# A diffusion layer in float32 on one core: its first phase written in a fixed order, some modulation chunks left unsplit, tiles given places

## The chip, the core and the metric

The kernel runs on one core of a Trainium2 chip. A core has a matmul engine (TensorE, PE in the profile; its weight loads are listed apart as PEld), two engines for element-wise work (VectorE, DVE, and ScalarE, ACT), a general engine (GpSimd, POOL) and an engine that here only issues DMA loads (SyncE, SP). Matmul results land in PSUM, which has 8 banks of 512 float32 columns; everything else lies in SBUF, 128 partitions wide. The metric is the time of one execution in microseconds on the device; less is better.

## What is computed

One layer over 256 latent tokens `x` and 256 context tokens `ctx`, width 2048, in float32, cut to what matters here:

```python
mod = silu(c) @ w_mod + b_mod                      # 6 x 2048 values; mod_c the same of c_ctx
sa, ca, ga, sm, cm, gm = split(mod, 6)
h   = rmsnorm(x)   * nw * (1 + ca)   + sa          # latent tokens
h_c = rmsnorm(ctx) * nw * (1 + ca_c) + sa_c        # context tokens
q, k, v, pool_in, gate_logits = h @ w_in           # of h_c only keys and values
q, k = rope(rmsnorm(q)), rope(rmsnorm(k))          # 16 half heads of 64
heads = (softmax(q1 k1) - lam * softmax(q2 k2)) @ v    # 8 heads, latent queries, all keys
y_a = rmsnorm(heads) @ w_a_up
y_b = (window means of 2, 4, 8, 16 tokens of pool_in - pool_in) @ pool_w @ w_b_up
x = x + ga * ((sigmoid(g_a) * y_a + sigmoid(g_b) * y_b) @ w_o)
x = x + gm * (relu(modulate(x, sm, cm) @ w_ff1) ** 2 @ w_ff2)
```

The first phase needs the parts `sa` and `ca` of the modulation, for both conditioning vectors at once, ahead of h and h_c.

## The kernel before

**Split products.** A float32 product is made from three matmuls in a faster, shorter format (f32r): each operand is split into a high and a low half, and high x high, high x low and low x high are summed in PSUM (`mm3`, lines 241 to 243). A 512 KB chunk of weights (128 x 1024) therefore goes through a chain: SP loads it into `raw` (5 buffers), ACT casts it to `whi` (line 213, 3 buffers), DVE subtracts to get `wlo` (line 214, 3 buffers), PE uses both. The order of all chunks is a list, `stream`, filled by `plan`; `wchunk` hands out the next one and keeps two more under way. 128 chunks of the later modulation parts bypass this: DVE multiplies them into a sum (`late_part`, line 588).

**First phase (0 to 171 us).** `w_m0` (2 x 4 chunks) and seven stretches of 8 chunks `w_m` give the modulation: the weights stream past `cv`, a stationary tile that holds silu(c) and silu(c_ctx) in halves in 4 of its 128 columns, so 4 rows of `mod` result (`mod_chunk`, line 347). After a stretch the rows are copied (`mod_rows`, line 352), turned into columns (`mod_columns`, line 359), combined with the biases in four DVE operations, and `hidden` makes tiles of h or h_c: per 256 columns a DVE scaling (line 380), an ACT addition that gives the high half (381), a DVE difference that gives the low half (382). Sums of squares for the two norms come from ACT, an addition (line 460; on DVE for x, on POOL for the context) and a matmul (461). Between the chunks stand steps of the first half of keys (4 tiles of 128 tokens) and of queries (2 tiles): a step is the three matmuls of one tile and one 128-row slice. Keys for h, queries and keys for h_c are separate generators that the table `carried` puts behind given chunks; the chunk of keys is kept in `first` until the context has used it too. Loads are in the order prm, x (4), `w_m0`, then chunks and context between.

**After it.** `qk_evac` normalizes and rotates keys and queries (POOL's sum at line 440) and queues a turn, the transposes of line 447, a given number of chunks later (`later`, `tick`). Then values group 0 (to about 210), queries, keys, values of group 1 (to 356), the pooling input `pin` (window sums on POOL, line 744; edges and difference in `pool_diff`, lines 756 to 760), gates `pg`/`pyy` (to 704), `w_o`, and the MLP in blocks (850 to 1512). `xstat` (lines 410 to 413) is the matmul loop with tokens stationary. In `pin`, the first ff1 block and ff1 (lines 939 and 942) it is the other way round: 128 columns of the weight chunk are the stationary side, tokens stream, 512 columns (both halves of h, line 939) or 256 (line 942). Attention is a side generator that the loop `run` advances by the matmuls counted (`scores` line 646, softmax 647 to 657, transposes 665, products with the values 674). A recording layer orders each engine's instructions as PSUM banks and buffers come free; `pin` keeps marked ones in the order of the code.

## Time and profile before

| | |
|---|---|
| median of 3 executions | 1519.9 us (1519.45 to 1520.57) |
| the profiled execution | 1519.78 us, its span 1517.7 us |
| outside the span | 2.1 us |
| PE / DVE / ACT / POOL busy | 98% / 70% / 50% / 9% |
| DMA, mean over the span | 229 GB/s |
| first phase | 0 to 171 us, with 17 matmuls of the values at its end |

The profile comes from the profiled execution; times in it are in us from the start of its span. A row of windows gives a stretch, its length, and for each engine the busy time with the count, then the clock that PE was granted (1 is full), the share of DMA time and the rate. A row of groups gives line, engine, operation, output and input tiles, shapes, count, busy time and mean ns of one, and the idle time before with what ended it. A timeline row gives the start, the duration, the operation and, in brackets, the wait ahead of it. Matmuls overlap: one of 512 columns takes some 390 ns from end to end while the next starts 227 ns after it.

### The profile page before, as it was taken

What the parts mean: (1) busy time and instruction counts of PE and PEld (TensorE: products, weight loads), DVE (VectorE), ACT (ScalarE), POOL (GpSimd) and SP (SyncE); (2) the same over time, 40 slices, a digit from 0 to 9 for tenths busy, and PEclk for the clock granted to TensorE, in tenths of its full rate; (3) what the DMA queues carried; (4) which work ended last, traced back from release to release, by engine and by line L of the source; (5) the groups of instructions that cost most, each with busy time, mean ns of one, the idle gap of its engine ahead of it and who ended that gap; (6) DMA issues with size and microseconds to landing.
All of it is one profiled execution on the core that took longest, in us unless ns stands there. A gap on an engine that the chain in (4) does not pass through costs nothing.

```text
span 1517.7 us, 19767 instructions
## 1 busy us (share of the span) xinstructions
PE 1480.7 (98%) x7336; PEld 1232.8 (81%) x7336; DVE 1063.2 (70%) x1280; ACT 755.7 (50%) x1007; POOL 129.3 (9%) x124
## 2 busy tenths in 40 slices
PE   7899999999989999999999999999999999999998
PEld 5677877768878888888879988888888888888887
DVE  7799878777887767666757665666666555555675
ACT  6677534556655444444444554544444454444432
POOL 0100111000140000000000100100000000000170
PEclk9899999999999999999999999999999999999999
DMA  8888668556568787788755677767777666666664
GB/s 314 310 283 308 214 215 285 177 167 193 167 216 300 254 275 272 242 295 296 235 181 168 220 251 245 232 217 244 231 241 240 202 188 193 193 187 193 184 200 142
DMA packets 97439, 347.82 MB, mean 229 GB/s; under 512 B 11072, under 2 KB 11712, under 8 KB 97344
## 3 DMA queue, kind: packets, MB, share of 16 engines
q1 hardware_dynamic: 96768, 345.49, 70.4%
q8 instruction: 57, 0.93, 0.3%
q0 software_dynamic: 576, 1.08, 0.2%
q14 instruction: 38, 0.31, 0.1%
HBM read 344.44 MB, written 2.10 MB: 228 GB/s over the span
## 4 chain that ended last, share of the span: by engine, by line
PE 88%; issue 3%; DVE 3%; DMA 3%; ACT 1%; POOL 1%; DVEq 0%; SPq 0%; ACTq 0%; POOLq 0%
PE f L939 14%; PE f L411 8%; PE f L410 8%; PE f L413 8%; PE f L942 7%; PE pg L413 4%; PE pg L410 4%; PE pg L411 4%; PE pyy L410 2%; PE wo L410 2%; PE wo L413 2%; PE wo L411 2%; PE pyy L413 2%; PE pyy L411 2%; PE v L411 2%
## 5 line engine op out<-in xcount | busy, mean ns | idle before, releaser
L214 DVE TENSOR_TENSOR wlo<-raw,whi 128x1024 fp32r<-128x1024 f32 x507 | 628.6, 1244 | 365.2 <-ACT whi L213 350.9
L213 ACT CAST whi<-raw 128x1024 fp32r<-128x1024 f32 x507 | 529.8, 1047 | 587.3 <-PE f L411 178.1
L939 PE MATMUL f<-h,whi 128*128 128x512 f32 x896 | 224.2, 392 | 0.0
L411 PE MATMUL f<-whi,act 128*128 128x512 f32 x512 | 199.3, 389 | 0.0
L410 PE MATMUL f<-whi,act 128*128 128x512 f32 x512 | 199.3, 389 | 0.0
L939 PEld LDWEIGHTS f<-h,whi 128*128 128x128 f32 x896 | 161.5, 189 | 29.1
L588 DVE SCALAR_TENSOR_TENSOR macc<-raw,sil,macc 128x1024 f32<-128x1024 f32 x128 | 166.2, 1299 | 1.4 <-DMA raw<-in_w_cm_dram 0.8
L413 PE MATMUL f<-wlo,act 128*128 128x512 f32 x512 | 136.8, 389 | 0.0
L942 PEld LDWEIGHTS f<-h,wlo 128*128 128x128 f32 x896 | 122.2, 190 | 8.7
L942 PE MATMUL f<-h,wlo 128*128 128x256 f32 x896 | 124.9, 282 | 0.0
L413 PEld LDWEIGHTS f<-wlo,act 128*128 128x128 f32 x512 | 96.1, 188 | 20.0
L411 PEld LDWEIGHTS f<-whi,act 128*128 128x128 f32 x512 | 96.1, 188 | 19.8
L410 PEld LDWEIGHTS f<-whi,act 128*128 128x128 f32 x512 | 96.1, 188 | 19.8
L410 PE MATMUL pg<-whi,hL 128*128 128x512 f32 x256 | 100.5, 393 | 0.0
L411 PE MATMUL pg<-whi,hL 128*128 128x512 f32 x256 | 99.7, 389 | 0.0
L950 POOL TENSOR_TENSOR rsq<-relu 128x512 f32<-128x512 f32 x28 | 29.2, 1042 | 537.6 <-ACT relu L949 516.7
L413 PE MATMUL pg<-wlo,hL 128*128 128x512 f32 x256 | 68.6, 390 | 2.5 <-DVE wlo L214 2.5
L413 PEld LDWEIGHTS pg<-wlo,hL 128*128 128x128 f32 x256 | 48.0, 188 | 12.9 <-DVE wlo L214 2.9
L410 PEld LDWEIGHTS pg<-whi,hL 128*128 128x128 f32 x256 | 48.1, 188 | 10.1 <-issue 0.2
L411 PEld LDWEIGHTS pg<-whi,hL 128*128 128x128 f32 x256 | 48.1, 188 | 10.1 <-issue 0.2
L410 PE MATMUL wo<-whi,mix 128*128 128x512 f32 x128 | 49.9, 390 | 0.0
L411 PE MATMUL wo<-whi,mix 128*128 128x512 f32 x128 | 49.8, 389 | 0.0
(267 smaller groups left out, 2205.1 us busy)
## 6 DMA issues: line engine op xcount, KB each, us to landing
raw<-in_w_ff_dram SPq DMA_DIRECT2D x240, 512.0 KB, 4.3
raw<-in_w_m_dram SPq DMA_DIRECT2D x64, 512.0 KB, 4.9
raw<-in_w_ga_dram SPq DMA_DIRECT2D x32, 512.0 KB, 4.6
raw<-in_w_cm_dram SPq DMA_DIRECT2D x32, 512.0 KB, 4.6
raw<-in_w_gb_in_dram SPq DMA_DIRECT2D x32, 512.0 KB, 4.5
raw<-in_w_ga_in_dram SPq DMA_DIRECT2D x32, 512.0 KB, 4.4
raw<-in_w_sm_dram SPq DMA_DIRECT2D x32, 512.0 KB, 4.7
raw<-in_w_o_dram SPq DMA_DIRECT2D x32, 512.0 KB, 4.6
```

Source lines behind the costliest of these rows:

```text
L213: act.copy(hi, raw)
L214: vec.tensor_sub(lo, raw, hi.bitcast(F32))
L410: pe.matmul(banks[t], tok(h, k, 0, tt), wt, start=k == 0, stop=False)
L411: pe.matmul(banks[t], tok(h, k, 1, tt), wt, start=False, stop=False)
L413: pe.matmul(banks[t], tok(h, k, 0, tt), wt, start=False, stop=k == 2 * nk - 1)
L588: pin(vec.scalar_tensor_tensor(acc, raw, sil[:, 0, k:k + 1], acc, ALU.mult, ALU.add))
L939: pe.matmul(ps, hi[:, kk * P:kk * P + P], both(h2, k), start=k == 0, stop=False)
L942: pe.matmul(ps[:, T:2 * T], lo[:, kk * P:kk * P + P], act_slice(h2, k, 0), start=False, stop=k == KT - 1)
L950: gp.tensor_mul(sq, r, r)
```

## The change

It rewrites the first phase and moves a few steps behind it.

1. All four engines and SP keep the order of the code until the phase ends (`ordered_all`). Tables say what follows which chunk: `STRETCHES` (loads), `then` (rows, turns, columns, hidden tiles, squares, tables), `PACE` (steps of keys and queries). Steps come from one queue, `side`, 96 in all. `w_m0`'s first half is loaded ahead of x; the context's squares are added on DVE.
2. In each stretch one chunk (two in the first three), ten in all, is not split: its float32 weights are used as they are, 4 matmuls of 256 columns, with the 2 columns of `sil` (float32) as the stationary side.
3. `scale_stream` multiplies x or the context in place by its norm, 512 columns at once; `hidden` then has one ACT operation per 256 columns with scale and bias, one ACT cast and one DVE subtraction for 512 columns, the latter after the next chunk (`low_halves`). Columns take three DVE operations.
4. `whi` and `wlo` are six tiles of 1028 columns with names of their own; chunks that serve as the stationary side (`w_p`, `w_ff1a`, `w_ff1`) start 4 columns (16 bytes) into theirs. The first queries' halves use the tag `aT`. Small constants and `small` tiles get places between the large ones.
5. Turns of the first keys and queries come one chunk later, the second half of `late_split` two, the window-16 `pool_diff` two. The rotation writes into the tiles that are there.

```diff
-    carried = {1: ((1, "kx", 0), (4, "q", 0)), 2: ((2, "kx", 1), (4, "q", 1)),
-               3: ((0, "kc", 0), (3, "kx", 2), (5, "q", 2), (6, "kc", 1))}
...
+    STRETCHES = [None,
+                 ("M0", "C0", "M1", "C1", "M2", "K0", "C2", "M3", "C3", "M4", "Q0", "M5", "M6", "M7"),
+                 ("M0", "M1", "M2", "K1", "M3", "M4", "Q1", "M5", "M6", "T0", "M7"),
+                 ("M0", "M1", "M2", "M3", "M4", "K2", "M5", "Q2", "M6", "M7")]
     for m in range(4, 8):
-        carried[m] = ((0, "kc", m - 2), (2, "kx", m - 1), (4, "q", m - 1))
-    carried[8] = ((0, "kc", 6), (0, "kx", 7), (0, "q", 7), (0, "kc", 7))
-    for m in range(9):
-        if m == 0:
-            for half in range(2):
-                for i in range(4):
-                    plan("w_m0", half, i)
-        for i in range(8 if m > 0 else 0):
-            if m < 8:
-                plan("w_m", m - 1, i)
-            for at, n, j in carried[m]:
-                if at == i and n != "kc":
-                    plan("w_k" if n == "kx" else "w_q", 0, j)
-            if m == 1 and i > 5 or m == 2 and i < 2:
-                plan("cT", (8 * m + i - 14))
-            if m == 3 and i == 4:
+        STRETCHES.append(("M0", "M1", "M2", f"K{m - 1}", "M3", "M4", f"Q{m - 1}", "M5", "M6", "M7"))
+    STRETCHES.append(("K7", "Q7"))
...
+    WHOLE = [None] + [(3, 5) if m < 4 else (3,) for m in range(1, 8)]
...
+    STATIONARY, OFFSET = ("w_p", "w_ff1a", "w_ff1"), 4
+    chunks = [0]
+
+    def halves(n, at):
+
+        i = chunks[0] % 3
+        chunks[0] += 1
+        return [pool.tile([P, 1028], F32R, tag=f"{part}{i}", name=part, bufs=1)[:, at:at + n] for part in ("whi", "wlo")]
...
+        if key[0] == "w_m" and key[2] in WHOLE[key[1] + 1]:
+            loaded.append((key, raw, raw))
+            return
...
+        elif key[:2] == ("w_q", 0):
+            hi, lo = [pool.tile([P, 1024], F32R, tag="aT", name=f"wq{part}", bufs=2) for part in ("hi", "lo")]
         else:
-            hi = pool.tile([P, n], F32R, tag="whi", name="whi", bufs=3)
-            lo = pool.tile([P, n], F32R, tag="wlo", name="wlo", bufs=3)
+            hi, lo = halves(n, OFFSET if key[0] in STATIONARY else 0)
...
+        while done[0] < len(loaded) and loaded[done[0]][1] is None:
+            done[0] += 1
+        while len(loaded) < len(stream) and sum(l[1] is not None for l in loaded[done[0]:]) < 1 + ahead:
+            load_next()
+            while done[0] < len(loaded) and loaded[done[0]][1] is None:
                 done[0] += 1
-                continue
-            load_next()
...
+    def mod_chunk(m, i, ps):
+
+        hi, lo = wchunk("w_m", m - 1, i)
+        if hi is lo:
+            for kk in range(2):
+                for c in range(0, 512, T):
+                    pe.matmul(ps[0:2, c:c + T], sil[:, :, 2 * i + kk], hi[:, kk * 512 + c:kk * 512 + c + T],
+                              start=False, stop=False)
+            return
...
+    def scale_stream(t, k):
+
+        src = (xT, cT)[t][:, k:k + 2, :]
+        vec.tensor_mul(src, src, rms[t].unsqueeze(1).broadcast_to([P, 2, T]))
...
     def hidden(k, t, c3, n=2):
 
         src, h = ((xT, hL), (cT, hC))[t]
         hw = work("hw", [P, n, T])
+        ht, k8 = h[k // 8], k % 8
         for kk in range(n):
-            ht, k8 = h[(k + kk) // 8], (k + kk) % 8
-            u = hw[:, kk, :]
-            bias = c3[:, n + kk, t:t + 1]
-            vec.scalar_tensor_tensor(u, src[:, k + kk, :], c3[:, kk, t:t + 1], rms[t], ALU.mult, ALU.mult)
-            act.activation(ht[:, 0, k8, :], u, AF.Identity, bias=bias)
-            vec.scalar_tensor_tensor(ht[:, 1, k8, :], u, bias, ht[:, 0, k8, :].bitcast(F32), ALU.add, ALU.subtract)
+            act.activation(hw[:, kk, :], src[:, k + kk, :], AF.Identity, bias=c3[:, n + kk, t:t + 1],
+                           scale=c3[:, kk, t:t + 1])
+        hi, lo = ht[:, 0, k8:k8 + n, :], ht[:, 1, k8:k8 + n, :]
+        act.copy(hi, hw)
+        lows.append(lambda: vec.tensor_sub(lo, hw, hi.bitcast(F32)))
 
     def tokens(nt):
         return [(hL, 0), (hL, 1), (hC, 0), (hC, 1)][:nt]
...
+    order = [("kx", 0), ("q", 0), ("kx", 1), ("q", 1), ("kc", 0), ("kc", 1), ("kx", 2), ("q", 2), ("kc", 2)]
+    for j in range(3, 8):
+        order += [("kx", j), ("q", j), ("kc", j)]
+    side = chain(*(pair_steps(*o) for o in order))
...
+        then.append({"M0": [lambda: take_rows(before)], "M1": [partial(turn_rows, k)],
+                     "M2": [partial(lambda k: hidden(k, 0, cols[k]), k)], "M3": [partial(scale_stream, 1, k)],
+                     "M5": [partial(lambda k: hidden(k, 1, cols[k]), k)],
+                     "M6": [partial(scale_stream, 0 if m < 7 else 1, k + 2)],
+                     "M7": [partial(tables, m - 3) if m < 6 else partial(scale_stream, 0, 14)] if m < 7 else []})
+    PACE = [None, (0, 0, 0, 0, 2, 2, 1, 1), (2, 0, 0, 0, 0, 2, 2, 2), (2, 2, 2, 2, 2, 2, 2, 1), (2, 1, 2, 2, 2, 2, 1, 1)]
+    PACE += [(2, 1, 1, 2, 2, 2, 1, 1)] * 3
...
+        before, ps = ps, bank("mod")
+        for step in STRETCHES[m]:
+            kind, i = step[0], int(step[1])
+            if kind in "KQ":
+                w = "w_k" if kind == "K" else "w_q"
+                held[w, i] = wchunk(w, 0, i)
+            elif kind == "M":
+                mod_chunk(m, i, ps)
+                low_halves()
+                for f in then[m].get(step, ()):
+                    f()
+                steps(PACE[m][i])
+    take_rows(ps)
...
-        qk_evac(kb[t], t, 0, kT, 2, 2 + t)
+        qk_evac(kb[t], t, 0, kT, 2, 3 + t)
     for t in range(2):
-        qk_evac(qb[t], t, 0, qT, 0, 6 + t)
+        qk_evac(qb[t], t, 0, qT, 0, 7 + t)
...
-            split(ah, al, acc[:, q * 512:q * 512 + 512])
-            later(4 + q, partial(late_sum, ah, al, norm_w[q] if norm_w else None, o[:, q * 512:q * 512 + 512]))
+            part = partial(late_half, q, acc, norm_w, o)
+            if q == 0:
+                part()
+            else:
+                later(2, part)
+                parts.append(waiting[-1])
+
+    def late_half(q, acc, norm_w, o):
+        ah, al = work("ah", dt=F32R), work("al", dt=F32R)
+        split(ah, al, acc[:, q * 512:q * 512 + 512])
+        later(3, partial(late_sum, ah, al, norm_w[q] if norm_w else None, o[:, q * 512:q * 512 + 512]))
...
-            later(3, partial(pool_diff, g, w, ps, sums))
+            later(3 if g < 3 else 5, partial(pool_diff, g, w, ps, sums))
```

What it does to the order of three places. PE in the first phase, the third stretch; `mod` are modulation matmuls, `w_k_2` and `w_k_3` the context's keys. Before:

```order
L347 MATMUL mod_600<-whi_638,cv_83 128x512 x2
L359 MATMUL modT_611<-prm_61,rows_598 128x4 x4
L241 MATMUL w_k_2_314<-first_281,hC0_96 128x512
L242 MATMUL w_k_2_314<-first_281,hC0_96 128x512
L243 MATMUL w_k_2_314<-first_281,hC0_96 128x512
L241 MATMUL w_k_3_315<-first_281,hC0_96 128x512
L242 MATMUL w_k_3_315<-first_281,hC0_96 128x512
L243 MATMUL w_k_3_315<-first_281,hC0_96 128x512
```

After (line 67 is that of the wrapper that pins an instruction):

```order
L67 MATMUL mod_908<-whi_891,cv_90 128x512 x2
L67 MATMUL mod_908<-wlo_892,cv_90 128x512 x2
L67 MATMUL modT_935<-prm_61,rows_919 128x4 x4
L67 MATMUL w_k_2_367<-first_302,hC0_100 128x512 x3
L67 MATMUL mod_908<-whi_911,cv_90 128x512 x2
L67 MATMUL mod_908<-wlo_912,cv_90 128x512 x2
L67 MATMUL w_k_3_368<-first_302,hC0_100 128x512 x3
L67 MATMUL mod_908<-raw_949,sil_79 2x256 x4
```

A chunk's high and low matmuls now stand together, one or two steps follow each, and the last row is an unsplit chunk.

PE at the end of the second value group (`v1`); `qkT` are turns of keys and queries, `sc` and `aTp` scores and transposes of attention, `late` sums of the later modulation. Before:

```order
L413 MATMUL v1_1_2678<-wlo_2684,hL0_94 128x512
L646 MATMUL sc_2785<-kT_1502,qT_1501 128x512
L665 MATMUL aTp_2797<-prm_61,e_2657 128x128 x4
L413 MATMUL v1_2_2679<-wlo_2684,hC0_96 128x512
L413 MATMUL v1_3_2680<-wlo_2684,hC0_96 128x512
L413 MATMUL v1_0_2677<-wlo_2684,hL0_94 128x512
L413 MATMUL v1_1_2678<-wlo_2684,hL0_94 128x512
L447 MATMUL qkT_2823<-prm_61,qm1_2587 128x128 x4
L413 MATMUL v1_2_2679<-wlo_2684,hC0_96 128x512
```

After:

```order
L469 MATMUL v1_3_2618<-wlo_2882,hC1_101 128x512 x2
L754 MATMUL sc_2724<-kT_1437,qT_1436 128x512
L773 MATMUL aTp_2736<-prm_61,e_2595 128x128 x4
L707 MATMUL late_2759<-ah_2489,ones_80 128x512
L708 MATMUL late_2759<-al_2490,ones_80 128x512
L501 MATMUL qkT_2763<-prm_61,qraw_2517 128x128 x4
L707 MATMUL late_2769<-ah_2625,ones_80 128x512
L708 MATMUL late_2769<-al_2626,ones_80 128x512
L501 MATMUL qkT_2808<-prm_61,qraw_2537 128x128 x4
L501 MATMUL qkT_2848<-prm_61,qraw_2557 128x128 x4
L501 MATMUL qkT_2893<-prm_61,qraw_2572 128x128 x4
```

Before, turns and attention stood among the matmuls of the values; now they follow the last of them in one row.

DVE at the window of 16 in the pooling; `za` are the window sums, `wlo` a chunk's split. Before:

```order
L238 TENSOR_TENSOR yb<-py,yb 128x512
L758 TENSOR_TENSOR za<-za,prm 128x7 x2
L214 TENSOR_TENSOR wlo<-raw,whi 128x1024
L756 TENSOR_TENSOR za<-za,prm 128x8
L760 SCALAR_TENSOR_TENSOR d<-za,pin 128x256
```

After:

```order
L866 TENSOR_TENSOR za<-za,prm 128x7
L235 TENSOR_TENSOR wlo<-raw,whi 128x1024
L688 SCALAR_TENSOR_TENSOR macc<-raw,sil,macc 128x1024
L235 TENSOR_TENSOR wlo<-raw,whi 128x1024
L260 TENSOR_TENSOR yb<-py,yb 128x512
L235 TENSOR_TENSOR wlo<-raw,whi 128x1024
L864 TENSOR_TENSOR za<-za,prm 128x8
L866 TENSOR_TENSOR za<-za,prm 128x7
```

The second edge product now stands behind three splits instead of ahead of one.

258 lines of the change are left out of this document (147 added, 111 removed).

## Prediction

> **What bounds the kernel now.** I read the page first (engine shares, slices, costliest groups), then the windows by stage, the waits of each stage, and the instructions around the waits.
>
> ```profile
> span 1517.7 us, 19767 instructions
> PE 1480.7 (98%) x7336; PEld 1232.8 (81%) x7336; DVE 1063.2 (70%) x1280; ACT 755.7 (50%) x1007; POOL 129.3 (9%) x124
> L214 DVE TENSOR_TENSOR wlo<-raw,whi 128x1024 fp32r<-128x1024 f32 x507 | 628.6, 1244 | 365.2 <-ACT whi L213 350.9
> L213 ACT CAST whi<-raw 128x1024 fp32r<-128x1024 f32 x507 | 529.8, 1047 | 587.3 <-PE f L411 178.1
> ```
>
> PE is busy 98% of the span: idle time to win back is 37 us in all, and beyond that only cheaper matmuls help. Every split costs a cast (1.05 us) and a subtraction (1.24 us), both beside PE as long as PE has other work. Where PE is not at its pace the windows tell:
>
> ```profile
> 0.00:25.00 25.00, 15.12 (x78) 11.89 (x78) 16.48 (x30) 17.82 (x26) 1.82 (x6) 1.00 0.91 322
> 25.00:45.00 20.00, 15.97 (x62) 10.40 (x62) 13.62 (x18) 11.63 (x15) 0.00 (x0) 1.00 0.92 339
> 45.00:56.00 11.00, 9.85 (x25) 6.02 (x25) 9.84 (x13) 9.31 (x17) 4.93 (x3) 0.53 0.74 263
> 132.80:149.40 16.60, 16.42 (x73) 12.61 (x72) 15.13 (x22) 12.78 (x17) 0.00 (x0) 1.00 0.90 316
> ...
> 0.00:57.50 57.50, 42.44 (x170) 29.56 (x171) 41.44 (x60) 40.26 (x57) 8.26 (x10) 0.91 0.88 317
> 57.50:171.00 113.50, 110.95 (x488) 86.98 (x487) 101.72 (x172) 78.64 (x108) 1.22 (x2) 1.00 0.82 284
> ```
>
> Columns: stretch, its length, busy us of PE, PEld, DVE, ACT, POOL, granted clock, DMA share, GB/s. The first 45 us have the DMA engines 91 to 92% busy: PE waits for weights. From 45 to 56 DMA falls to 263 GB/s and the clock to 0.53. After that PE is near full, DVE close behind (15.1 of 16.6 us).
>
> **Part 1, the first phase: -5 us.** What was left for PE at 57.5 us in the kernel before, and the price of a step:
>
> ```profile
> L347 PE MATMUL mod<-wlo,cv 128*128 128x512 f32 x90 | 28.4, 395 | 0.9 <-DVE wlo L214 0.7
> L347 PE MATMUL mod<-whi,cv 128*128 128x512 f32 x90 | 28.2, 393 | 0.2 <-ACT whi L213 0.2
> L241 PE MATMUL w_k<-first,hC 128*128 128x512 f32 x32 | 12.9, 402 | 0.0
> L241 PE MATMUL w_q<-whi,hL 128*128 128x512 f32 x28 | 11.0, 398 | 0.0
> L241 PE MATMUL w_k<-first,hL 128*128 128x512 f32 x26 | 10.5, 409 | 0.1
> L359 PE MATMUL modT<-prm,rows 4*128 4x4 f32 x24 | 2.4, 203 | 1.2 <-ACT rows L352 1.2
> L461 PE MATMUL ssq<-sq,mean 128*128 128x256 f32 x8 | 2.0, 378 | 0.0
> ...
> 440.48 1.07 PE L413 MATMUL pg<-wlo,hL 128*128 128x512 f32 x4
> 441.39 0.39 PE L410 MATMUL pg<-whi,hL 128*128 128x512 f32 x1
> 293.46 1.89 PE L674 MATMUL ob<-aT,v 128*128 128x256 f32 x8
> ```
>
> Four matmuls of 512 columns start in 0.91 us (440.48 to 441.39): 0.227 each, so 0.91 for a modulation chunk (four) and 0.68 for a step of keys or queries (three: lines 241, 242, 243). Left at 57.5 us: 180 matmuls of modulation (45 chunks), 86 steps, turns and sums of squares 4 us, together 40.9 + 58.5 + 4 = 103.4. The stretch to 171.0 also holds 17 matmuls of the values (3.9), so the first phase ends at an equivalent of 167.1, and of those 109.6 us about 6 are lost.
>
> The changed kernel needs by the end of its second stretch x and the context (8 loads), 8 + 16 modulation chunks and 4 of keys and queries: 36 loads of 512 KB and the constants, 19 MB. At 317 to 339 GB/s (rows above) that is 56 to 60 us; I take 57.5. Nothing else holds it up longer: of those 24 chunks 4 need no split, and the squares of the context leave POOL, which stood in DVE's way:
>
> ```profile
> 54.85 4.53 DVE L214 TENSOR_TENSOR wlo<-raw,whi 128x1024 fp32r<-128x1024 f32 x2
> ...
> 53.87 4.43 POOL L460 TENSOR_TENSOR sq<-sq 128x512 f32<-128x512 f32 x2 [1.16 <-DVE wlo L214]
> ```
>
> Two splits that are 1.24 each took 4.53 beside POOL. Then 40 chunks and 82 steps are left. An unsplit chunk is four float32 matmuls of 256 columns; line 674, the nearest, leaves two records per matmul, eight in 1.89 us, so (1.89 - 0.39)/7 = 0.214 a record and 1.71 a chunk, 0.8 more than split. Their stationary side here is 2 wide, which no row shows: at the least they cost what two f32r matmuls do, 0.45 a chunk, so -0.5 to +0.8; I take 0.8, the row of the same kind. Six of the ten lie behind 57.5: 34 x 0.91 + 6 x 1.71 + 82 x 0.68 + 2.5 (turns) = 99.5. For losses I take 4.7 rather than 6, the waits at the phase's end (rows, turn, columns, hidden) among them, since one split and about 1.3 us of hidden() leave DVE in each stretch (below). End: 57.5 + 99.5 + 4.7 = 161.7 against 167.1; I round to 5. Bounds: all loads at 339 GB/s and no losses but 1, -10; no lead at 57.5, the six unsplit chunks 4.9 dearer, losses 1.9 smaller, +3.
>
> The small edits there: hidden() per stretch was four scalings and four differences
>
> ```profile
> L380 DVE SCALAR_TENSOR_TENSOR hw<-xT,col,aT 128x256 f32<-128x256 f32 x16 | 7.1, 479 | 0.2
> L382 DVE SCALAR_TENSOR_TENSOR hL<-hw,col,hL 128x256 fp32r<-128x256 f32 x16 | 8.1, 541 | 0.0
> L460 DVE TENSOR_TENSOR sq<-sq 128x512 f32<-128x512 f32 x4 | 2.8, 692 | 4.3 <-ACT sq L459 4.3
> ```
>
> on DVE, 4 x (0.48 + 0.54) = 4.1, and is now four operations on 512 columns, 4 x 0.69 = 2.8; ACT gains two casts of 512 columns (between 0.5 and 1.05, half the 1024-column row above), which its 12.8 of 16.6 us carry. PE then has 7 x 0.91 + 1.71 + 12 x 0.68 + 0.5 = 16.7 us a stretch, DVE about 14: PE becomes the bound, hence no gain from shorter DVE work. With everything in program order, a step that needs a late hidden tile holds all behind it on PE; the halves are queued one chunk early, so I put it at nothing, and at a few us if it fails (in the +3). x's loads go behind four chunks on SP: x is wanted only after half 0, while DMA is full either way. An unsplit chunk keeps its load buffer until PE is done with it; DMA, 82% busy after 57.5 us, can wait for that. The tables, in three pieces, move the same work.
>
> **Part 2, two waits behind it: -5.5 us.**
>
> ```profile
> PE qkT L447 <- POOL qm L440: 3.0, 2, 2.0
> PE pg L413 <- DVE wlo L214: 2.5, 1, 2.5
> ...
> 444.45 0.17 DVE L758 TENSOR_TENSOR za<-za,prm 128x7 f32<-128x7 f32 x1 [2.87 <-POOL za L744]
> ```
>
> The turn of the keys waits 3.0 us for POOL's sum; one chunk later (24 matmuls, over 5 us) that is done: -3, at worst 0 if another wait is late there. The second wait is a chain: DVE stands 2.87 us at the window-16 edge for POOL's sums, a split is queued behind it, and PE waits 2.5 us for that split. Two chunks later all but one of those edge products stand behind further splits: -2.5, at worst 0.
>
> **Part 3, the end of the second value group: +5 us.** The new order places a score of attention, in the order of PSUM banks, behind the last value matmul, and with it eight turns and three units of attention, which before were spread among the matmuls. They wait there for each other:
>
> ```profile
> L651 ACT ACTIVATE e<-sc,mx 128x512 f32<-128x512 f32 x32 | 21.9, 686 | 23.7 <-DVE mx L647 23.5 <-issue 0.2
> L448 ACT COPY kT<-qkT 128x512 f32<-128x512 f32 x8 | 4.7, 585 | 1.9 <-PE qkT L447 1.9
> L616 ACT COPY v<-v 128x512 f32<-128x512 f32 x8 | 4.1, 592 | 0.0
> L647 DVE TENSOR_REDUCE mx<-sc 128x1 f32<-128x512 f32 x32 | 21.1, 683 | 2.6 <-PE sc L646 2.6
> L657 DVE SCALAR_TENSOR_TENSOR e<-e,rs 128x512 f32<-128x512 f32 x16 | 13.0, 814 | 11.6 <-ACT e L656 11.6
> ```
>
> One unit's chain from score to transpose is two maxima (1.37), the last exponential (0.69), ACT's scaling (about 0.7) and the sum (0.81): 3.6 us, with copies of keys and values (0.59 each, four and four) ahead of it on ACT. PE has some 0.5 us of its own between two units. One uncovered chain and a part of the copies make 5; at least 0 (matmuls of the next stage can come up in between), at most 7 with two chains.
>
> **Part 4, where tiles lie: -7 us.** Chunks used as the stationary side start 16 bytes further, and every large tile has its own place. No row shows an address. What it could touch are matmuls that are slower than their columns:
>
> ```profile
> 863.17 1.12 PE L942 MATMUL f<-h,wlo 128*128 128x256 f32 x8
> 864.12 2.00 PE L939 MATMUL f<-h,whi 128*128 128x512 f32 x8
> ...
> L241 PE MATMUL pin<-hL,whi 128*128 128x256 f32 x128 | 37.5, 293 | 0.0
> L241 PE MATMUL f<-h,whi 128*128 128x256 f32 x128 | 37.3, 296 | 0.7 <-ACT h L65 0.7
> ```
>
> After eight of 256 columns the next starts 0.95 us later: 0.119 each where half of 0.227 is 0.1135, so the weights' load, not the columns, sets the pace. That is 896 matmuls (56 blocks of 16) x 5.5 ns = 5 us; their 896 partners of 512 columns are 2.0 us for eight with the last at 0.39, 0.230, so 3 ns x 896 = 2.7; the pooling input and the first ff1 block, 3 x 128 each (lines 241 to 243), 768 x 6.5 ns = 5. If loads came down to the columns' pace, 13 us; if addresses do nothing, 0. I take the middle, and 0 and -13 as ends.
>
> The Trainium skill, "SBUF — State Buffer", section Who interferes with whom, gives PE one read port for the moving operand and an independent one for weight loads, which wait on nobody. By it no placement changes a matmul, the fourth term is 0 and the sum -5.5; the rows show that 256 columns take 0.119 rather than 0.1135, not why.
>
> **Sum.** -5 - 3 - 2.5 + 5 - 7 = -12.5. The profiled execution took 1519.78, 0.1 under the median of 1519.9 and 2.1 over its own span, so 1519.8 - 12.5 = **1507**.
>
> **Rivals.** (a) Placement does nothing: the other terms stand, -5.5, so 1514 (1509 to 1518 with their ends). For it: the two groups of line 241 read different tiles at different places and take 293 and 296 ns. Against: the 6 ns over the columns' pace have no other cause in view. It is also the answer of the page named above.
>
> (b) Slower: PE becomes the bound of the first phase. The ten unsplit chunks cost 8 us where PE has no idle time to hide them; if x arriving later uses up the early lead, the phase ends 3 us later, the bunch of attention takes 7, the turns and the pool wait give back 5.5 at most, and placement 0: +4.5, so 1524. It decides if PE is still at 11 modulation chunks at 57.5 us (56 less the 45 left). Against it: the first 57.5 us hold 15 us in which PE idles, and loading order alone fills some of them.
>
> (c) All goes well: the phase's losses vanish (-10), the bunch costs nothing, placement gives 10 of 13, the two waits 5.5: -25, so 1495. For it: each waiting engine named above is one that the change relieves.
>
> **How the numbers follow.** Forecast (1501 to 1512) 0.45, (a) 0.30, (b) 0.10, (c) 0.15. A measurement here can tell about 0.2%, 3 us, from no change. Faster by more: the forecast, (c) and two thirds of (a), 0.80; the rest of (a) and a little of (b) within, 0.11; slower 0.09. The range 1495 to 1520 takes in (a) and nearly all of the forecast and leaves out half of (c) and most of (b).
>
> **What would show it.** Right: the first phase's last step near 162; the window 45 to 56 at full clock and over 300 GB/s; no wait of the turns on POOL and none of the gates' matmuls at the pool's edge; new waits of aTp on ACT and DVE before the pooling input; ff1 under 0.119 and 0.230 a matmul. Wrong: ff1 blocks of unchanged length (then (a)); stretches of over 17 us or a phase that ends past 168 (then (b)); an unsplit chunk at other than 1.7 us.

## The result and the profile after

| | median, us | runs | ratio to before, 95% interval |
|---|---|---|---|
| before | 1520.2 | 4 (1519.5 to 1521.1) | |
| changed | 1539.2 | 4 (1534.8 to 1541.1) | 1.012 (1.0098 to 1.0143) |

The change costs 19 us where 13 were to be won. The profiled execution of the changed kernel took 1541.05, the longest of the four, so the stages below add up to some 2 us more than the medians; its span is 1539.3. First the page and the windows that answer to those of before; the columns are as there.

```profile
span 1539.3 us, 19767 instructions
PE 1496.6 (97%) x7376; PEld 1238.5 (80%) x7376; DVE 1046.6 (68%) x1235; ACT 755.4 (49%) x1015; POOL 122.4 (8%) x120
```

```profile
0.00:25.00 25.00, 16.01 (x78) 14.29 (x78) 16.10 (x27) 16.34 (x24) 1.82 (x6) 0.93 0.91 343
25.00:45.00 20.00, 15.62 (x44) 8.36 (x45) 14.25 (x20) 15.02 (x23) 0.00 (x0) 0.74 0.92 337
45.00:57.50 12.50, 12.50 (x55) 9.59 (x53) 6.28 (x8) 5.02 (x8) 0.00 (x0) 1.00 0.66 218
57.50:183.50 126.00, 121.62 (x516) 87.05 (x516) 93.18 (x140) 85.10 (x123) 0.00 (x0) 0.97 0.80 274
359.00:379.20 20.20, 15.11 (x62) 7.85 (x61) 9.17 (x18) 15.63 (x35) 2.64 (x3) 0.83 0.18 53
```

PE's busy time has grown by 16 us. The 40 records more are those of the ten unsplit chunks, eight each where a split chunk has four; at 0.9 to 1.0 us more a chunk they are 9 to 10 us of it. The rest goes with a lower clock, 0.986 over the span where the kernel before has 0.994: slower work, not idleness. DVE is less busy, as intended, and it does not help. From 45 to 57.5 us PE is full while loading falls to 218 GB/s: PE has become the bound there. The last row is the end of the second value group, to the first matmul of the pooling input: 20 us where the kernel before needs 1.8.

Following the first and last matmuls of each stage through both traces gives where the time went (us from the start of the span; the end of the first phase is less the value matmuls that stand in it, at 0.227):

| | before | changed | behind by | gained or lost here |
|---|---|---|---|---|
| first phase ends | 167.3 | 181.1 | 13.8 | +13.8 |
| queries of group 1 start | 217.2 | 227.6 | 10.4 | -3.4 |
| last value matmul starts | 356.0 | 358.7 | 2.7 | -7.7 |
| pooling input starts | 357.8 | 379.2 | 21.4 | +18.7 |
| gates start | 430.0 | 455.8 | 25.8 | +4.4 |
| products behind the gates start | 460.1 | 483.4 | 23.3 | -2.5 |
| ff1 blocks start | 850.2 | 875.2 | 25.0 | +1.7 |
| last matmul ends | 1513.2 | 1534.8 | 21.6 | -3.4 |

The values end only 2.7 us late because attention, which stands among them in the kernel before, has been put off: the -7.7 and the +18.7 belong together and make 11, with the pooling 15.4. So there are two losses, the first phase and the bunch, and smaller gains, the clearest at the end.

What PE waits for between 356 and 480 us in the changed kernel (where the kernel before has its wait of the gates on a split and one of a transpose):

```profile
PE pin L265 <- DVE wlo L235: 4.8, 2, 3.0
PE sc L754 <- ACT kT L502: 4.4, 1, 4.4
PE pd L265 <- DVE wlo L235: 0.7, 1, 0.7
PE osum L793 <- POOL osq L789: 0.7, 1, 0.7
PE qkT L501 <- ACT e L759: 0.6, 1, 0.6
```

The gates no longer wait; the pooling input does, and a score waits 4.4 us for the keys' copies. And the bunch itself, PE's instructions in order of time:

```profile
358.05 1.07 PE L469 MATMUL v<-wlo,hC 128*128 128x512 f32 x4
359.04 1.12 PE L754 MATMUL sc<-kT,qT 64*128 64x512 f32 x2
360.10 0.66 PE L773 MATMUL aTp<-prm,e 128*128 128x128 f32 x4
...
364.25 0.66 PE L501 MATMUL qkT<-prm,qraw 128*128 128x128 f32 x4 [0.62 <-ACT e L759]
369.35 2.08 PE L754 MATMUL sc<-kT,qT 64*128 64x512 f32 x4 [4.44 <-ACT kT L502]
371.36 1.11 PE L773 MATMUL aTp<-prm,e 128*128 128x128 f32 x4
372.27 1.91 PE L793 MATMUL osum<-osq,mean 128*128 128x512 f32 x2
374.11 1.37 PE L754 MATMUL sc<-kT,qT 64*128 64x512 f32 x4
...
379.20 0.37 PE L263 MATMUL pin<-hL,whi 128*128 128x256 f32 x1
```

Behind the wait of 4.44 everything is slow: four scores take 2.08 where the next four take 1.37, with the clock at 0.83 over the stretch.

The ff1 blocks, the same two rows as before:

```profile
888.02 1.11 PE L1050 MATMUL f<-h,wlo 128*128 128x256 f32 x8
888.97 1.98 PE L1047 MATMUL f<-h,whi 128*128 128x512 f32 x8
890.78 1.11 PE L1050 MATMUL f<-h,wlo 128*128 128x256 f32 x8
```

Eight of 512 columns now start in 1.81 us rather than 1.84, so 0.226 each, no longer above the columns' pace; those of 256 still take 0.119.

### The profile page after: what moved, and what is told of

Same layout as the page of the kernel before. It is cut to its first block, busy times and chain, and to the rows that moved or that the text cites. A ratio compares the mean times of both kernels' runs of the same rounds, so it can differ in the third digit from the quotient of the medians.

```text
span 1539.3 us, 19767 instructions
## 1 busy us (share of the span) xinstructions
PE 1496.6 (97%) x7376; PEld 1238.5 (80%) x7376; DVE 1046.6 (68%) x1235; ACT 755.4 (49%) x1015; POOL 122.4 (8%) x120
## 4 chain that ended last, share of the span: by engine, by line
PE 67%; DVE 1%; ACT 1%; issue 0%; DVEq 0%; ACTq 0%
PE f L1047 13%; PE f L467 8%; PE f L466 8%; PE f L469 8%; PE f L1050 7%; PE pg L466 3%; PE pg L467 3%; PE pg L469 3%; PE wo L469 2%; PE wo L466 2%; PE wo L467 2%; PE pyy L466 2%; PE pyy L467 2%; PE pyy L469 2%; PE f L263 1%; PE f L265 1%
## 5 line engine op out<-in xcount | busy, mean ns | idle before, releaser
L235 DVE TENSOR_TENSOR wlo<-raw,whi 128x1024 fp32r<-128x1024 f32 (+1 forms) x435 | 538.9, 1241 | 372.7 <-ACT whi L234 340.0
L234 ACT CAST whi<-raw 128x1024 fp32r<-128x1024 f32 (+1 forms) x435 | 455.4, 1048 | 597.4 <-PE f L467 184.8
L67 DVE TENSOR_TENSOR wlo<-raw,whi 128x1024 fp32r<-128x1024 f32 x55 | 66.4, 1222 | 30.9 <-ACT whi L67 30.3
L67 ACT CAST whi<-raw 128x1024 fp32r<-128x1024 f32 x55 | 56.5, 1045 | 19.8 <-DMA raw<-in_w_m_dram 11.6
```

Source lines behind the costliest of these rows:

```text
L67: return (lambda *a, **k: pin(emit(*a, **k))) if any(f[0] for f in self.flags) else emit
L234: act.copy(hi, raw)
L235: vec.tensor_sub(lo, raw, hi.bitcast(F32))
```

## The experiments

The theory from the traces, called A here, is one of separate mechanisms, each with its place: the bunch (made by where the later modulation's sums fall), the unsplit chunks (PE is the bound), the queue on ACT at the end of the phase, the fixed order, the context loaded early. The rivals stand in each expectation: that the bunch only shows work that has to be paid for anyway, that the saved casts are worth the dearer matmuls, that data arrive no sooner whatever the order. Medians are of 4 to 11 runs, the kernel before on the same chips at 1518.9 to 1520.0. One kernel's times spread by up to 8 us, so differences under 2 us are not read. The changed kernel stands in its own series alone, and its ratio is known to 1.0098 to 1.0143; what a single edit gained against it is therefore given by the ratios to the kernel before as well.

**The bunch alone.**

```diff
-        later(3, partial(late_sum, ah, al, norm_w[q] if norm_w else None, o[:, q * 512:q * 512 + 512]))
+        later(2, partial(late_sum, ah, al, norm_w[q] if norm_w else None, o[:, q * 512:q * 512 + 512]))
```

> The changed kernel with one number altered: the sums of the later modulation are queued two chunks after their split, not three, so that they stand among the value matmuls and attention is spread again. Theory 1 (the bunch at the end of the second value group is a cost of its own and comes from where these sums take PSUM banks): the pooling input starts at most 3 us after the last value matmul rather than 20, and the time falls by 10 to 14 us, to 1525 to 1529. Theory 2 (attention has to be paid for somewhere, the bunch only shows it at one place): the values take longer by what the bunch takes less, and the time stays within 3 us of 1539.

Measured: 1525.7 (1521.9 to 1529.7), ratio to before 1.0044 (1.0028 to 1.006), so 13.5 us below the changed kernel by the medians and 11.6 by the ratios. PE at the end of the values:

```profile
363.87 1.07 PE L469 MATMUL v<-wlo,hC 128*128 128x512 f32 x4
364.87 1.13 PE L754 MATMUL sc<-kT,qT 64*128 64x512 f32 x4
365.93 0.66 PE L773 MATMUL aTp<-prm,e 128*128 128x128 f32 x4
366.34 0.37 PE L263 MATMUL pin<-hL,whi 128*128 128x256 f32 x1
```

The pooling input starts 1.8 us after the last of the values, as in the kernel before, and the stage from the end of the first phase to it is 11.0 us shorter (184.8 for 195.8), the pooling 4.5. One number in a queue that has nothing to do with attention cost 12 to 13 us: attention was not paid for elsewhere.

**The unsplit chunks, and the end of the phase.** Each alone in the changed kernel:

```diff
-    WHOLE = [None] + [(3, 5) if m < 4 else (3,) for m in range(1, 8)]
+    WHOLE = [None] + [() for m in range(1, 8)]
```

> The changed kernel with all modulation chunks split (no unsplit chunk). Theory 1 (PE bounds the first phase, an unsplit chunk costs it 0.9 us more than a split one): the first phase ends 8 to 9 us sooner, near 174, and the time falls as much, to about 1530. Theory 2 (without unsplit chunks ACT and DVE become the bound of the stretches, as the change supposes): the phase ends within 3 us of 183, the time is 1536 to 1542.

```diff
-        hi, lo = wchunk("w_m", m - 1, i)
+        hi, lo = wchunk("w_m", m - 1, i, ahead=1 if (m, i) == (7, 7) else AHEAD)
```

> The changed kernel with one chunk less of lookahead at the last modulation chunk, so that on ACT the copy of the last rows no longer stands behind the cast of the last query chunk, which waits for a buffer that PE holds. Theory 1 (this queue makes the wait of 2.6 us at 164 and the low clock behind it): the wait falls under 1 us, the clock stays full, the phase ends 4 to 5 us sooner, 1534 to 1535. Theory 2 (the wait is the chain rows, turn, columns, hidden tile itself): the gap moves behind the turn and the end stays within 1.5 us.

Measured: all split 1534.0 (1532.9 to 1535.0), the phase ends at 174.7 (counted as in the table above, where the changed kernel has 181.1); less lookahead 1534.5 (1532.9 to 1536.9), at 176.7. So 5.2 and 4.6 us by the medians, but 3.3 and 2.6 by the ratios (1.0098 and 1.0103), whose intervals overlap with the changed kernel's: on theory A's side, the first less than expected, neither clear of the noise by its time alone. The end of the phase in the changed kernel and with less lookahead:

```profile
166.73 0.58 PE L67 MATMUL modT<-prm,rows 4*128 4x4 f32 x4 [2.58 <-ACT rows L67]
167.25 5.49 PE L67 MATMUL w_k<-first,hC 128*128 128x512 f32 x12
```

```profile
165.00 0.41 PE L67 MATMUL modT<-prm,rows 4*128 4x4 f32 x4
165.33 2.99 PE L67 MATMUL w_k<-first,hC 128*128 128x512 f32 x12
```

On ACT the copy of the rows stood behind two casts, of a value chunk and of the last query chunk, and the first of them waited for the buffer that PE gives back with its last step: PE had nothing left but the turn of those rows. The wait cost 2.6 us, and the twelve matmuls behind it ran at half clock (5.49 for 2.99).

The low clock does not follow each time. The first phase is the same in the kernel with later sums sooner and in the one with the offset taken back (below). Both have the wait, 2.3 us; in the first the twelve matmuls take 4.61 and the phase ends at 179.2, in the second they run at full clock and it ends at 177.1:

```profile
165.57 0.41 PE L67 MATMUL modT<-prm,rows 4*128 4x4 f32 x4 [2.25 <-ACT rows L67]
165.91 3.00 PE L67 MATMUL w_k<-first,hC 128*128 128x512 f32 x12
```

So up to 4 us of the 181.1 are that execution's clock. The queue costs 2.3 to 2.6 us of wait and up to 3.4 more by the clock; against the 176.7 without it the three ends are 0.4 to 4.4 us later.

**Placement, taken back.**

```diff
-    STATIONARY, OFFSET = ("w_p", "w_ff1a", "w_ff1"), 4
+    STATIONARY, OFFSET = ("w_p", "w_ff1a", "w_ff1"), 0
```

> The changed kernel with chunks that serve as the stationary side starting at the tile's start, not 16 bytes into it; all else as changed. Theory 1 (the offset is what makes the matmuls of ff1 cheaper): the eight ff1 blocks grow by 3.5 us in all, to what they were in the kernel before, 1542 to 1543. Theory 2 (the tiles' new places do it, or the two operands' turns in time): the ff1 blocks stay as short as in the changed kernel, the time within 1 us of it.

Measured: 1540.9 (1539.5 to 1542.8), 1.7 us above the changed kernel; from the first ff1 block to the end the traces have 663.0 us, without the edit 659.6 and in the kernel before 663.1. The time is less clear than the stage, but the stage says 3.4 us and gives the rows of the kernel before back:

```profile
L1047 PE MATMUL f<-h,whi 128*128 128x512 f32 x896 | 224.1, 392 | 0.0
...
L1050 PE MATMUL f<-h,wlo 128*128 128x256 f32 x896 | 124.9, 282 | 0.0
```

The 16 bytes do it, not the new places of the tiles.

**Three edits at once, then the clock, then the order.** The three edits above (later sums, all split, less lookahead) together:

```diff
-        later(3, partial(late_sum, ah, al, norm_w[q] if norm_w else None, o[:, q * 512:q * 512 + 512]))
+        later(2, partial(late_sum, ah, al, norm_w[q] if norm_w else None, o[:, q * 512:q * 512 + 512]))
-    WHOLE = [None] + [(3, 5) if m < 4 else (3,) for m in range(1, 8)]
+    WHOLE = [None] + [() for m in range(1, 8)]
-        hi, lo = wchunk("w_m", m - 1, i)
+        hi, lo = wchunk("w_m", m - 1, i, ahead=1 if (m, i) == (7, 7) else AHEAD)
```

> The changed kernel with three edits at once: later sums two chunks after their split, all modulation chunks split, one chunk less of lookahead at the end of the first phase. Theory 1 (three separate costs that add): 1539 less 13.5, 5.2 and 4.6, so 1514 to 1517, faster than the kernel before by 3 to 5 us. Theory 2 (the costs share a cause, such as the low clock, and hide one another): 1519 to 1523.

Measured: 1520.4 (1519.0 to 1521.8), ratio 1.0003 (0.9994 to 1.0012): back to the kernel before, not past it. The time is in theory 2's range, but that is no sign that the costs hide one another: theory 1's figures were taken from medians of two series. By the medians it is 18.8 us of the 23.3 that the single edits add up to; by the ratios it is 17.8 (1.0120 to 1.0003) where the single edits give 11.6, 3.3 and 2.6, together 17.5. As far as the noise lets it be told, the costs add. The casts of the chunks that are split again bring a wait of 1.5 us at 61 us with a low clock behind it; the kernel with only the chunks split has it too (1.54 us), so it is part of what that edit gains less than expected.

```diff
+    def warm(n):
+        for _ in range(n):
+            pe.matmul(sb[:, T:2 * T], cv[:, 0, :], cv[:, 0:2, :].rearrange("p a t -> p (a t)"), start=True, stop=True)
+    warm(16)
...
+             "M4": [partial(warm, 12), partial(squares, 1)],
```

> The kernel with the three edits, and 28 more matmuls without use in the first 45 us, 16 behind the first modulation chunks and 12 ahead of the context's sums, where PE waits for a cast and for DVE; their result is not read. Theory 1 (the early lead is missing because waits of about 2 us let the clock fall to half for the 10 us behind them): the clock in 30 to 47 us stays above 0.95 and the first phase ends 3 to 5 us sooner than with the three edits alone. Theory 2 (weights arrive too late, whatever the clock): the clock stays up and the end within 1 us.

Measured: 1519.5 (1517.6 to 1522.9). The same window, first with the three edits, then with the added matmuls:

```profile
30.00:47.00 17.00, 14.76 (x43) 9.74 (x42) 14.61 (x19) 13.53 (x21) 0.00 (x0) 0.70 0.94 330
```

```profile
30.00:47.00 17.00, 14.62 (x59) 10.74 (x58) 15.29 (x19) 13.80 (x22) 0.00 (x0) 0.90 0.91 327
```

The clock rises from 0.70 to 0.90, not to the 0.95 that both theories took for granted, and the time moves by 0.9 us, under what can be read. So the low clock is not the main thing that holds the start; the added matmuls take PE time themselves, and what a full clock alone would bring is not shown.

```diff
-    ordered_all[0] = True
+    ordered_all[0] = False
```

> The kernel with the three edits, the first phase no longer held to the order of the code, so that each engine's order is chosen as in the kernel before. Theory 1 (the fixed order itself costs nothing, its places of casts and chunks do): within 2 us of the kernel with the three edits. Theory 2 (the fixed order is what lost the lead, since PE stands behind a late operand though other steps are ready): the phase ends 4 us or more sooner.

Measured, in the kernel with the three edits: 1515.2 (1513.4 to 1516.8), ratio 0.9971 (0.996 to 0.9982). The phase ends at 168.0 where it was 174.0. Theory 2: with all chunks split the fixed order costs 5.2 us. At 57.5 us the two stand within a chunk of each other; behind it the fixed order has 3.4 us lost to half clock after the wait at 61 us and some 3 us more in waits and late starts of its matmuls. That other steps were ready then follows from the order, no run shows it apart.

**The offset in the kernel before.**

```diff
+            at = 4 if key[0] in ("w_p", "w_ff1a", "w_ff1") else 0
-            hi = pool.tile([P, n], F32R, tag="whi", name="whi", bufs=3)
-            lo = pool.tile([P, n], F32R, tag="wlo", name="wlo", bufs=3)
+            hi = pool.tile([P, 1028], F32R, tag="whi", name="whi", bufs=3)[:, at:at + n]
+            lo = pool.tile([P, 1028], F32R, tag="wlo", name="wlo", bufs=3)[:, at:at + n]
```

> The kernel before with one thing of the change: chunks that serve as the stationary side start 16 bytes into their tiles. Theory 1 (the offset shortens ff1 by itself): the ff1 blocks are 3.4 us shorter in all, the time near 1516. Theory 2 (offset and the new places act together only): 1519 to 1521.

Measured: 1535.0 (1534.0 to 1536.6), ratio 1.0101: 16 us slower, outside both. The edit did more than it meant to. Wider tiles move the next ones, so that, worked out from the tile sizes in the code (no trace shows an address), five of the six halves no longer start at the same remainder of 256 bytes as the other large tiles, the chunks that stream among them:

```profile
L412 PE MATMUL f<-whi,act 128*128 128x512 f32 x512 | 201.0, 393 | 0.0
L411 PE MATMUL f<-whi,act 128*128 128x512 f32 x512 | 200.9, 392 | 0.0
L414 PE MATMUL f<-wlo,act 128*128 128x512 f32 x512 | 139.9, 395 | 0.0
```

These are the matmuls of ff2, 389 ns each in both kernels of the study; by starts they are 230 to 233 apart on average rather than 227. To see whether the place of the streamed chunk matters by itself, all chunks got the 16 bytes, in the kernel with the three edits and the free order, where the six tiles keep their places:

```diff
-            hi, lo = halves(n, OFFSET if key[0] in STATIONARY else 0)
+            hi, lo = halves(n, OFFSET)
```

> The kernel with the three edits and the free order, with every chunk 16 bytes into its tile, those that stream through PE too. Theory 1 (the weights and the tokens are read at the same time, and only their distance counts, whichever is stationary): ff2, gates and the output projection stay at 227 ns a matmul or gain, the end within 1 us. Theory 2 (a streamed chunk that lies off the place of the other large tiles is slowed, as in the kernel before with wider tiles): 229 to 234 ns, the time 5 to 15 us longer.

Measured: 1532.2 (1530.8 to 1532.5), 17 us above that kernel, 2 us more than theory 2's range.

```profile
L466 PE MATMUL f<-whi,act 128*128 128x512 f32 x512 | 202.0, 395 | 0.0
L467 PE MATMUL f<-whi,act 128*128 128x512 f32 x512 | 201.5, 393 | 0.0
L469 PE MATMUL f<-wlo,act 128*128 128x512 f32 x512 | 139.4, 394 | 0.0
```

16 bytes help a chunk that is loaded as the stationary side (0.229 to 0.227) and harm one that streams (0.227 to 0.231 or 0.232). Theory 2; which reads or writes meet there is not told by these runs.

**The unsplit chunks in a free order.** The kernel with the three edits and the free order, with the ten unsplit chunks back:

```diff
-    WHOLE = [None] + [() for m in range(1, 8)]
+    WHOLE = [None] + [(3, 5) if m < 4 else (3,) for m in range(1, 8)]
```

> The kernel with the three edits and the free order, but with the ten unsplit chunks back, to see their price where each engine's order is chosen freely. Theory 1 (an unsplit chunk is dearer for PE and PE bounds the phase): the phase ends 4 to 8 us later, 1519 to 1523. Theory 2 (in a free order the ten casts and subtractions saved are worth as much as PE's extra time): 1514 to 1517.

Measured: 1522.8 (1521.2 to 1524.7), 7.6 us more; the phase ends at 176.7 for 168.0. Of the 9 to 10 us that ten unsplit chunks cost PE, the saved casts and subtractions bring back little here; in the fixed order, where splitting them gained 3 to 5 us, they bring back about half. And 176.7 is also where the phase ends in the fixed order with less lookahead and unsplit chunks: with these in place, the free order gains nothing.

**The context's loads.** The kernel with the three edits and the free order, with the four context loads after chunks 6 and 7 of the first stretch and 0 and 1 of the second, and the squares with what hangs on them moved into the second stretch:

```diff
-                 ("M0", "C0", "M1", "C1", "M2", "K0", "C2", "M3", "C3", "M4", "Q0", "M5", "M6", "M7"),
-                 ("M0", "M1", "M2", "K1", "M3", "M4", "Q1", "M5", "M6", "T0", "M7"),
+                 ("M0", "M1", "M2", "K0", "M3", "M4", "Q0", "M5", "M6", "C0", "M7", "C1"),
+                 ("M0", "C2", "M1", "C3", "M2", "K1", "M3", "M4", "Q1", "M5", "M6", "T0", "M7"),
...
```

> The kernel with the three edits and the free order, with the context's four loads and its squares moved back to the end of the first and the start of the second stretch, as in the kernel before. Theory 1 (the lead is missing because 2.1 MB of context are loaded while loading is the limit, ahead of chunks that PE could use): PE has done 7 to 8 modulation chunks at 45 us rather than 5, and the phase ends 2 to 4 us sooner, 1511 to 1513. Theory 2 (all of it has to be loaded anyway and PE catches up): more chunks at 45 us, but the end within 1 us.

Measured: 1511.2 (1507.8 to 1511.8), ratio 0.9937 (0.9924 to 0.995), faster than the kernel before by 0.6%. Counted from PE's records at 45 us: 8.8 chunks and 8 steps, where the kernel before has 8.0 and 8, the changed one 5.5 and 2, the one with early context and free order 5.2 and 2. The window from 25 to 45 us with early and with late context, both in the free order:

```profile
25.00:45.00 20.00, 11.70 (x31) 7.21 (x32) 18.88 (x27) 14.14 (x22) 0.00 (x0) 0.66 0.91 334
```

```profile
25.00:45.00 20.00, 15.49 (x59) 9.99 (x59) 17.38 (x25) 12.78 (x19) 0.00 (x0) 0.98 0.97 361
```

The rate differs by 8%, PE's work by far more: what comes is what PE can use. The edit moves the loads and the squares together; which of them counts can be read from PE's longest wait with the early context and the cast that ended it:

```profile
38.55 1.22 PE L389 MATMUL mod<-whi,cv 128*128 128x512 f32 x2 [5.55 <-ACT whi L234]
```

```profile
33.82 3.74 ACT L513 ACTIVATE sq<-cT 128x512 f32<-128x512 f32 x7
37.47 1.03 ACT L234 CAST whi<-raw 128x1024 fp32r<-128x1024 f32 x1
```

In the trace's records of the loads, the chunk of that cast landed at 36.76, behind the four context loads (30.71, 31.98, 33.27 and 35.47). So the squares, which ACT worked on until 37.5, hold it up by 0.7 us at most, and the loads by the rest. At 57.5 us the lead of the late context has shrunk to 1.8 chunks and a third of a step, 1.8 us. The other 3 of the 4.9 us by which the phase ends sooner (163.1 for 168.0) come after that, where PE idles 0.9 us rather than 3.2; that these too come from the loads is not shown.

**Turns and pool edge, taken back** in that fastest kernel (the delays of the kernel before):

```diff
-        qk_evac(kb[t], t, 0, kT, 2, 3 + t)
+        qk_evac(kb[t], t, 0, kT, 2, 2 + t)
-        qk_evac(qb[t], t, 0, qT, 0, 7 + t)
+        qk_evac(qb[t], t, 0, qT, 0, 6 + t)
-            later(3 if g < 3 else 5, partial(pool_diff, g, w, ps, sums))
+            later(3, partial(pool_diff, g, w, ps, sums))
```

> The fastest kernel so far (three edits, free order, context late) with the turns of the first keys and queries one chunk sooner and the window-16 differences two chunks sooner again, as in the kernel before. Theory 1 (both terms as predicted: 3.0 us of waits of the turns on POOL and 2.5 us at the pool's edge come back): 1516 to 1517. Theory 2 (the edge's wait only moved to another split, so that only the turns' wait comes back): 3 us more, about 1514, with a wait of about 2.5 us at the gates in place of the one in the pooling input.

Measured: 1509.7 (1509.0 to 1512.1), ratio 0.9936 (0.9922 to 0.9949). Neither theory: nothing comes back. PE's waits from 163 to 460 us:

```profile
PE pin L265 <- DVE wlo L235: 2.3, 1, 2.3
PE aTp L772 <- ACT e L758: 1.9, 1, 1.9
...
PE qkT L501 <- POOL qraw L494: 0.4, 1, 0.4
```

The turns wait 0.4 us for POOL without the later turn, and the wait of 2.3 on a split is in the pooling input with either delay.

## Why the prediction was wrong

Its sum was -12.5; measured is +19. Term by term, the stages as the traces have them:

**First phase: -5 forecast, +13.8 in the trace, outside its bounds of -10 to +3.** The step that failed is the lead that the load sum gave: "36 loads of 512 KB ... that is 56 to 60 us; I take 57.5. Nothing else holds it up longer". Loading did run at 337 to 343 GB/s to 45 us, but of the 15 MB that came, 2.1 were context, which gives PE little to do, and PE's own time was not counted there. By 57.5 us 18.0 MB had come, close to the sum's 19; it is "Nothing else holds it up longer" that did not hold. PE had done 11 modulation chunks by then, not 16, and 8 steps, not 14. What is left then can be summed as the prediction did for the kernel before:

```profile
L67 PE MATMUL mod<-wlo,cv 128*128 128x512 f32 x75 | 24.0, 399 | 0.2
L67 PE MATMUL mod<-whi,cv 128*128 128x512 f32 x74 | 23.2, 394 | 0.0
L67 PE MATMUL mod<-raw,sil 128*2 128x256 f32 x64 | 15.1, 379 | 0.0
```

```profile
76.50 1.89 PE L67 MATMUL mod<-raw,sil 128*2 128x256 f32 x8
78.32 1.65 PE L67 MATMUL w_k<-first,hC 128*128 128x512 f32 x6
79.81 0.62 PE L67 MATMUL mod<-whi,cv 128*128 128x512 f32 x2
...
86.43 1.52 PE L67 MATMUL w_k<-first,hL 128*128 128x512 f32 x6
87.79 0.62 PE L67 MATMUL mod<-whi,cv 128*128 128x512 f32 x2
```

149 matmuls of split chunks at 0.227, eight unsplit chunks at 1.82 (76.50 to 78.32), 88 steps at 0.68 and 3 for the turns are 111.3, with 2.5 of values 113.8 of the 126.0 us to 183.5: losses of 12.2 where I took 4.7. So of the 19.4 us between the forecast end, 161.7, and 181.1, 11.8 are work that was still left at 57.5 us, and 7.5 are losses.

The assumption "no lead" was the rival's, with a chance of 0.10, and its sign came true as stated: PE still at 11 chunks at 57.5 us. It priced this at +3, with six unsplit chunks behind 57.5 us where eight are left without a lead, and with losses smaller by 1.9; they doubled. That they would not grow was the second failure: "with everything in program order, a step that needs a late hidden tile holds all behind it ... I put it at nothing". It holds for the hidden tiles (one wait of 0.5 us) and not for the copy of the last rows: that wait of 2.58 us and the 6.8 us at half clock behind it, 3.4 us lost, are 6.0 of the 12.2, and the rest is what the kernel before loses. In the two other traces with this first phase the phase ends at 179.2 and 177.1, so the stage is +10 to +14. The 5.2 us of the fixed order belong to the kernel with all chunks split; with the unsplit ones the free order ends the phase at the same 176.7.

Against the kernel before, which stood at 11 chunks and 10 steps at 57.5 us, the start is only 1.4 of the +13.8 (two steps): most of it is the eight unsplit chunks, 7.3, and that last wait with its clock, 6.0; the rest is -0.9. By the ends of the phase in the profiles: 163.1 in the fastest kernel, 168.0 with the context early, 174.0 in the fixed order too, 176.7 with the unsplit chunks as well and 181.1 with the longer lookahead on top.

**The unsplit chunk: 0.8 forecast, 1.0 measured** at full clock (1.82 for 0.91, and two steps right behind it take 1.49, from 78.32, where two others take 1.36, from 86.43). Right in kind: "PE becomes the bound, hence no gain from shorter DVE work" fits what is lost with them in the free order, 7.6 us; it holds less in the fixed order, where the split chunks bring waits of their own.

**Turns and pool edge: -5.5 forecast.** The stage of the first values did become 3.4 us shorter, and the gates' wait is gone. But both edits taken back cost nothing in the fastest kernel, so the gain was most likely not theirs (whose it was, no run shows), and at the pool's edge the wait had only moved from the gates to the pooling input. "-2.5, at worst 0": it is the worst.

**The bunch: +5 forecast, bound 7, measured 13.5 by the medians, 11.6 by the ratios.** The place, the order and the chain were right. The size failed at "PE has some 0.5 us of its own between two units. One uncovered chain and a part of the copies make 5": besides the wait of 4.4 us on copies, the low clock behind it and the two units that run bare, the later order of the pooling pays 4.4 more, which no bound held. Its cause is one delay in the queue of the later modulation's sums, which the prediction did not name; that these reach attention through the order in which PSUM banks come round is argued from the order, not shown.

**Placement: -7 forecast, -3.4 measured, bounds 0 to -13.** Mostly the 512-column partners came down (3 ns x 896 = 2.7; the narrow ones give 0.8 ns x 896 = 0.7); the narrow ones stay at 0.118 to 0.119, so what keeps them above 0.1135 is not what the offset touches. The Trainium skill, "SBUF — State Buffer", Who interferes with whom, gives PE two independent read ports and says that PE never waits on anyone. By that the term would be 0; the runs say otherwise, since the same program is 3.4 us faster in its last stages with 16 bytes more on the chunks that are stationary, and 17 us slower with them on those that stream. Whether it is PE's two reads that meet, or a read and another engine's access, is not shown.

Of the rivals, (b) came nearest: slower, by its mechanism and its mark at 57.5 us, at 1524. That it stopped 15 us short is again the bunch and the losses.

## What to carry to other kernels

Early in a kernel that waits for its loads, ask of each load what the bound engine can do with it: 2.1 MB of context, landed 6 to 9 us sooner than in the fastest kernel, cost 4 us in the free order, and a sum of bytes alone does not show it. An edit that spares an engine that is not the bound at the price of the one that is loses most of that price, here 7.6 us for ten chunks in the free order, and still 3 to 5 in the fixed order, where the spared engines do hold PE up at times. And a delay in one queue can reorder another that shares buffers with it: look in the order for work that has come to stand in a row, and price the low clock behind its first wait too. A stage that ends on such a wait varies by some 4 us from one execution to the next, so a stage is better read from several traces than from one.

## What the runs showed of the hardware

Where a tile starts changes the pace of matmuls that read it: where the weight chunk streams, 512 columns start every 227 ns with the chunk at its tile's start and every 231 to 232 with it 16 bytes further; where the chunk is the stationary side it is 229 to 230 at the start and 227 with it 16 bytes further. A wait of 1.88 us in the changed kernel, with shorter ones of 0.6 and 0.5 beside it, was followed by half clock (0.74 over 25 to 45 us). The wait of 2.3 to 2.6 us at the last turn of rows was followed by 6.8 us of half clock in the changed kernel, by 3.4 in the one with later sums sooner and by none in the one with the offset taken back (granted clock from 165 to 175 us: 0.66, 0.83 and 1.00): such a wait does not always lower the clock. The Trainium skill, "TensorE: Matmul & The Clock Gate", What's actually happening, has the clock fall after an idle window of some 3.4 us; here several shorter waits in a row were enough, at times. What the places of other engines' tiles do at the same time stays open.
